# Weight pieces of the next head group tied one product earlier, and cached-key steps taken out of the changeover, in a gated-parallel decoder step on one core

## The chip, the cores and the metric

The kernel runs on one core of a Trainium2 chip. The metric is the device time of one launch in microseconds (us); the time before is the median of three timed runs, and the profile is one further execution.

## The reference

One decoder layer is applied to 1024 prompt tokens and to 64 sample tokens (8 sequences of 8 tokens, each behind a cache), all in float32:

```
u = rmsnorm(x);  [a | q | k | v | g_a | g_b] = u @ w_in
A = (multi-scale causal pooling of a, one linear map per group, scale) @ w_pa
B = (attention, 3 head groups of 4 heads, head width 64, (window, dilation) = (128,1), (512,4), (2048,16);
     q and k normed per head; the groups' outputs weighted by their softmax denominators) @ w_pb
h = x + (sigmoid(g_a) * A + sigmoid(g_b) * B) @ w_o
y = h + relu(rmsnorm(h) @ w_up)^2 @ w_down
```

The sample tokens read cached keys and values of each head group; for the group with window 2048 every sample row has 64 cached keys of its own per head. The updated caches are outputs too.

## The kernel before

All large products are made from float32 weights that are split into two parts: `panel` loads 256 columns of a weight matrix in four pieces of 256 KB into a ring of three `raw` buffers (line 119, a DMA issued by SP), and `split` writes the high part on ACT (line 108) and the remainder on DVE (line 109) into one of three `places`. A product is then three passes, 24 matmuls for a block of 128 tokens and 256 columns (`gemm`, line 147).

The attention stage runs over the head groups in the order 2, 1, 0 (line 921). Each group needs three panels, `load(0)` for q, `load(1)` for k, `load(2)` for v, and uses them for nine token blocks: block 8 holds the 64 sample rows (24 matmuls of lines 527 and 530), blocks 0 to 7 the prompt. The three places hold exactly one group's q, k and v, so the next group's q panel overwrites the q weights now in use, and so on. Products are written as (group, block, j) with j = 0, 1, 2 for q, k, v. In groups 2 and 1 the last two blocks go together, in the order (6,0), (7,0), (6,1), (7,1), (6,2), (7,2); the next group begins with blocks 8 and 0: (8,0), (0,0), (8,1), (0,1), (8,2), (0,2).

`load(j, after)` ties the split of each of the four pieces behind a named product of TensorE (`behind_pe`). A raw buffer comes free when its piece is split, and the SP queue issues its DMAs in the order in which they stand, so a DMA whose buffer isn't free holds those behind it. The order of PE is written out by hand; that of the other engines and of SP is made by a scheduler from the program.

Beside the products runs the work on the cached keys and values of group 2's sample rows: `sample_own_keys` is a generator, and each call of `own_step` (line 969) takes it one step on. A step issues the two DMAs of a piece of 256 KB (`pck` for keys, `pcv` for values, a ring of two buffers, line 719), four multiplications on POOL (line 733 or 757) and sums on DVE (lines 735, 760, 761). It needs 35 calls; groups 1 and 0 offer 19 each, one behind each product or pair of products of a prompt block. After the attention come the gate products (`pga`, `pgb`), whose panels `ga`, `gb` use the same ring and places, then output projection and feed-forward (`ph`, `pz`, `py`), which run from about 400 us of the span to its end.

Other names: `nat` are token blocks copied into order for group 0; `qs`, `wq`, `wrow` are small operands loaded at the start of group 1; `ms` and `mr` are the head norms (sum on DVE line 549, power on POOL line 550), with which ACT scales q and k (line 555) before PE transposes them (`tqg`, line 570); `sg` are scores, `smg` the exponentials (ACT line 596), `tpg` their transposes, `pog` the products with v, `ocg` their copies (line 620).

```
            load(0, (h, 6, 1), (h, 7, 1), (h, 6, 2), (h, 6, 2))
            load(1, (h, 6, 2), (h, 7, 2), (h, 7, 2), (h, 7, 2))
```

stand before a group's loop (h is the group before it), and `load(2, ...)` behind the products (8,0) and (0,0).

Of the kernel before, what the change touches and what calls it, by code (L numbers as in the profile page):

```python
# [32 lines left out]
def decoder_step(ctx, tc, i, o):  # L33
# [78 lines left out]
    def panel(src, name, between=None, after=None):  # L112

        n = src.shape[1]
        wt = places[:, place[0] % 3]
        place[0] += 1
        for a in range(0, n, 512):
            raw = rr(wp, [P, 512], F32, name=f"raw_{name}_{a}", tag="raw", bufs=3)
            dma(raw, src[:, a:a + 512])
            if between is not None:  # L120
                between(a // 512)
            ins = split(wt[:, 0, a:a + 512], wt[:, 1, a:a + 512], raw)
            if after is not None:
                behind_pe(ins, after[a // 512])
        throttle.append(ins)
        return wt
# [257 lines left out]
    def flush():  # L384
        while later:
            later.pop(0)()
# [36 lines left out]
    def pool_branch():  # L423
        res = []
        for g in range(4):
            yield from pooling(g, res)
            if g == 3:
                soon(lambda: (behind_pe(dma_st(o["pool_prompt"].rearrange("g p t -> p g t"), ends)),
                              behind_pe(dma_st(o["pool_sample"].rearrange("g p b t -> p g (b t)"), states))))
            start(pool_linear(g, *res[g]), ("p", g), now=True)  # L430
# [26 lines left out]
    def start(gen, tag, now=False, first=False):  # L457
        def run():
            yield from gen
            done.add(tag)  # L460
        if now:
            r = run()
            next(r)
            active.append(r)
        else:
            waiting.insert(0 if first else len(waiting), run())
# [18 lines left out]
    def qkv_tiles(name, sample):  # L485
        qk = rr(ap1, [P, 512], F32, name=f"qk{name}", tag="qk", bufs=2)
        if sample:
            return qk, ap1.tile([P, 256], F32, name=f"v{name}", tag="vs")
        return qk, rr(ap, [P, 256], F32, name=f"v{name}", tag="v", bufs=4)
# [12 lines left out]
    def in_order(blk):  # L502

        for s, copy in ((1, s_.copy), (0, v_.tensor_copy)):
            for k in range(0, KD, 2):
                t = rr(np_, [P, 2, P], F32R, name=f"nat{blk}_{s}{k}", tag=f"nat{s}{k}", bufs=1)
                copy(t.rearrange("p k (l r) -> p k l r", r=4),
                     act_t[s].rearrange("p k (r l) -> p k l r", r=4)[:, k:k + 2, blk * 32:(blk + 1) * 32, :].bitcast(F32))
                nat[s, k], nat[s, k + 1] = t[:, 0, :], t[:, 1, :]
# [381 lines left out]
    def own_step(every):  # L891
        count[0] += 1
        if count[0] % every == 0:
            if next(own_keys, True) is not None and (2, "own") not in done:
                done.add((2, "own"))
# [25 lines left out]
    for g in (2, 1, 0):  # L921
        nq = i["qk_norm"]
        if g == 1:
            assert ("p", 3) in done
            flush()
            pa.close()
            pam.close()
            ap2 = pb2.enter_context(tc.tile_pool(name="att2", bufs=1, reuse_waits="tile"))
            sp1 = psm.enter_context(tc.tile_pool(name="smp1", bufs=1, side="right", reuse_waits="tile"))
            np_ = psm2.enter_context(tc.tile_pool(name="nat", bufs=1, side="right", reuse_waits="tile"))  # L930
            sp = psm2.enter_context(tc.tile_pool(name="smp2", bufs=1, side="right", reuse_waits="tile"))
            osm = ap2.tile([P, 3, 4, 66], F32, name="osm")

            for a in range(2):
                v_.memset(osm[64:, a], 0.0)
                v_.memset(osm[64:, a, :, 64], -NEG)
            qs = sp1.tile([P, 768], F32, name="qs")
            for hf in range(2):
                dma(qs[64 * hf:64 * hf + 64], new_d[2].rearrange("t b c -> (t b) c"))
            wq = sp1.tile([P, 2, 256], F32, name="wq", tag="ss")[:, 0]  # L940
            dma(wq, bass.AP(tensor=nq.tensor, offset=nq.offset + 2 * 512, ap=[[0, P], [1, 256]]))
            v_.scalar_tensor_tensor(qs[:, :256], wq, HD ** -0.5, qs[:, :256], op0=ALU.mult, op1=ALU.mult)
            own_keys = sample_own_keys(qs)
        wrow = ap1.tile([P, 256], F32, name=f"wrow{g}", tag="wrow")
        dma(wrow, bass.AP(tensor=nq.tensor, offset=nq.offset + g * 512 + 256, ap=[[0, P], [1, 256]]))
        wts = [(place[0] + j) % 3 for j in range(3)]

        def load(j, *after):
            panel(i["w_in"][2 + 3 * j + g], f"qkv{g}_{j}", after=[ends_of[a] for a in after] or None)


        if g == 2:
            load(0)
            load(1)
            load(2)
        else:
            h = g + 1
            load(0, (h, 6, 1), (h, 7, 1), (h, 6, 2), (h, 6, 2))
            load(1, (h, 6, 2), (h, 7, 2), (h, 7, 2), (h, 7, 2))
        for blks in ((8, 0), (1,), (2,), (3,), (4,), (5,)) + (((6, 7),) if g else ((6,), (7,))):  # L960
            if g == 1 and 6 in blks:
                in_order(0)
            tiles = {b: qkv_tiles(f"{g}_{b}", b == 8) for b in blks}

            for js in (((0, 1), (2,)) if blks[0] in (1, 2, 3, 4, 5) else ((0,), (1,), (2,))):
                for b in blks:
                    qkv_part(g, wts, b, f"{g}_{b}", tiles[b], js)
                    if g < 2 and b < 8:
                        own_step(1)
                    if 2 in js:  # L970
                        (sample_block if b == 8 else prompt_block)(g, b, *tiles[b])
                if g == 2 and 2 in js and 8 in blks:
                    start(pool_branch(), "p", now=True)
                if g < 2 and 0 in js and 8 in blks:
                    load(2, (g, 8, 0), (g, 0, 0), (g, 0, 0), (g, 0, 0))


    while (2, "own") not in done:
# [327 lines left out]
```

## Time and profile before

| what | value |
|---|---|
| time, median of 3 runs | 1546.94 us (1546.55 to 1548.58) |
| profiled execution | 1541.33 us, span 1539.6 us |
| granted TensorE clock, mean over the span | 0.996 |
| HBM read, written | 155.54 MB, 65.10 MB |
| DMA issues of qkv weight pieces | 36 of 256 KB |
| cached pieces `pck`, `pcv` | 32 issues each, 256 KB |

The profiled execution was 5.61 us shorter than the median of the timed runs. Rows of a timeline give the start and the length in us, the engine, the line and operation, the tile written and those read, and in brackets how long the engine stood idle before it and what released it. `SPq` is the issue queue of SP. PE is TensorE's matmul, PEld its weight load.

### The profile page before, as it was taken

Reading aid. Unit: us, or ns where it says so; the run is one execution under the profiler, and the core shown is the slowest. Engines: PE = TensorE matmul, PEld = TensorE weight load, DVE = VectorE, ACT = ScalarE, POOL = GpSimd, SP = SyncE. Lnnn points to the kernel's source line nnn. Section 1 sums busy time; section 2 is a strip of 40 time slices with the busy share of each in tenths; the row PEclk is TensorE's granted clock in tenths of the full one; section 3 lists DMA queues with packets and bytes.
Section 4 is the critical chain, followed back from the end, with each engine's and each line's share of the span. In section 5 each row is a group of like instructions: output and inputs, shape, how many; then the busy total and the mean of one; then the engine's idle time right before and its main releaser. Section 6 shows DMA issues by size and latency. Waiting matters only on the chain.

```text
span 1539.6 us, 25519 instructions
## 1 busy us (share of the span) xinstructions
PE 1518.6 (99%) x9785; PEld 1473.3 (96%) x9785; DVE 880.1 (57%) x1948; ACT 521.0 (34%) x1613; POOL 202.5 (13%) x245
## 2 busy tenths in 40 slices
PE   9999899899999999999999999999999999999998
PEld 8989788778999999999999999999999999999998
DVE  7655555868745434344575555555555555655556
ACT  8567655677853232222341111111111211112100
POOL 1611256555100000010010000000000000000000
PEclk9999899999999999999999999999999999999999
DMA  5312676765344453584231331312312213223002
GB/s 199 105 51 73 183 180 167 215 163 136 108 144 161 153 173 108 172 253 169 73 107 54 107 100 60 106 65 95 106 61 99 100 64 109 75 89 106 29 7 116
DMA packets 104535, 178.64 MB, mean 116 GB/s; under 512 B 16919, under 2 KB 69725, under 8 KB 103198
## 3 DMA queue, kind: packets, MB, share of 16 engines
q1 hardware_dynamic: 98302, 126.70, 26.6%
q0 software_dynamic: 6112, 50.33, 9.7%
q8 instruction: 76, 1.25, 0.3%
q14 instruction: 45, 0.37, 0.1%
HBM read 155.54 MB, written 65.10 MB: 143 GB/s over the span
## 4 chain that ended last, share of the span: by engine, by line
PE 92%; DMA 3%; DVE 2%; ACT 1%; SPq 1%; issue 1%; POOL 0%; DVEq 0%; POOLq 0%; ACTq 0%
PE py L147 25%; PE pz L147 24%; PE pgb L147 6%; PE ph L147 6%; PE pqk L147 6%; PE pga L147 5%; PE pv L147 4%; PE pa L147 3%; PE a L261 3%; PE pb L147 2%; DMA raw_qkv<-in_w_in_dram 1%; PE pq L147 1%; PE pk L147 1%; PE pog0b L617 1%; PE sg0b L586 1%
## 5 line engine op out<-in xcount | busy, mean ns | idle before, releaser
L147 PE MATMUL pz<-act,places 128*128 128x384 f32 (+1 forms) x2304 | 382.4, 326 | 0.0
L147 PE MATMUL py<-z,places 128*128 128x384 f32 (+1 forms) x2304 | 381.6, 327 | 0.0
L147 PEld LDWEIGHTS pz<-act,places 128*128 128x128 f32 x2304 | 379.5, 188 | 0.4
L147 PEld LDWEIGHTS py<-z,places 128*128 128x128 f32 x2304 | 379.7, 188 | 0.0
L1193 DVE TENSOR_TENSOR y<-y,py 128x384 f32<-128x384 f32 (+1 forms) x360 | 188.3, 531 | 112.9 <-PE py L147 112.0
L1175 ACT ACTIVATE z<-r 128x384 fp32r<-128x384 f32 (+1 forms) x96 | 48.7, 509 | 323.3 <-DVE r L1174 323.3
L1174 DVE SCALAR_TENSOR_TENSOR r<-pz,rbh 128x384 f32<-128x384 f32 (+1 forms) x96 | 51.2, 535 | 172.5 <-PE pz L147 172.5
L1204 POOL DMA_DIRECT2D out_kv_sample_dram<-in_cache_kv_dram x44 | 21.8, 496 | 933.7 <-ACT places L108 912.4
L108 ACT ACTIVATE places<-raw_u 128x512 fp32r<-128x512 f32 x64 | 38.4, 627 | 266.9 <-PE py L147 260.1
L147 PE MATMUL pga<-act,places 128*128 128x384 f32 (+1 forms) x576 | 98.0, 328 | 0.0
L147 PE MATMUL pgb<-act,places 128*128 128x384 f32 (+1 forms) x576 | 97.8, 326 | 0.0
L147 PE MATMUL ph<-act,places 128*128 128x384 f32 (+1 forms) x576 | 95.9, 327 | 0.0
L147 PEld LDWEIGHTS pgb<-act,places 128*128 128x128 f32 x576 | 95.4, 188 | 0.0
L147 PEld LDWEIGHTS ph<-act,places 128*128 128x128 f32 x576 | 94.8, 188 | 0.3
L147 PEld LDWEIGHTS pga<-act,places 128*128 128x128 f32 x576 | 94.6, 188 | 0.3
L550 POOL TENSOR_TENSOR mr<-ms,mhalf 128x4 f32<-128x4 f32 (+2 forms) x39 | 49.6, 1273 | 107.6 <-DVE ms L549 102.0
L147 PE MATMUL pqk<-places,act 128*128 128x512 f32 x240 | 60.7, 402 | 0.0
L1177 DVE TENSOR_TENSOR z<-q,z 128x384 fp32r<-128x384 f32 (+1 forms) x96 | 51.3, 535 | 8.1
L109 DVE TENSOR_TENSOR places<-raw_d,places 128x512 fp32r<-128x512 f32 x64 | 41.4, 689 | 22.7 <-ACT places L108 22.6
L147 PEld LDWEIGHTS pqk<-places,act 128*128 128x128 f32 x240 | 44.5, 191 | 9.8 <-issue 0.2
L733 POOL TENSOR_TENSOR pck<-pck,qs 128x256 f32<-128x256 f32 x64 | 47.3, 770 | 43.5 <-DMA pck<-in_cache_kv_dram 16.6
L1176 DVE TENSOR_TENSOR q<-r 128x384 f32<-128x384 f32 (+1 forms) x96 | 51.3, 535 | 2.7
(296 smaller groups left out, 2039.7 us busy)
## 6 DMA issues: line engine op xcount, KB each, us to landing
out_kv_sample_dram<-in_cache_kv_dram POOLq DMA_DIRECT2D x36, 960.0 KB, 5.8
raw_u<-in_w_up_dram SPq DMA_DIRECT2D x64, 256.0 KB
raw_d<-in_w_down_dram SPq DMA_DIRECT2D x64, 256.0 KB
raw_qkv<-in_w_in_dram SPq DMA_DIRECT2D x36, 256.0 KB
pck<-in_cache_kv_dram SPq DMA_DIRECT2D x32, 256.0 KB
pcv<-in_cache_kv_dram SPq DMA_DIRECT2D x32, 256.0 KB
out_kv_sample_dram<-in_cache_kv_dram POOLq DMA_DIRECT2D x8, 1008.0 KB, 5.4
kts<-in_kT_dram SPq DMA_DIRECT2D x20, 256.0 KB
```

Of the source, the lines that this page charges most:

```text
L108: ins = s_.activation(dst_hi, src, AF.Copy)
L109: v_.tensor_tensor(dst_lo, src, dst_hi.bitcast(F32), op=ALU.subtract)
L147: last_mm[0] = t_.matmul(out, lhs(a, k), rhs(b, k), start=(j == 0), stop=(j == len(terms) - 1))
L261: last_mm[0] = t_.matmul(pts[m][:, :n], wt[:, a, kk, m * P:(m + 1) * P], act4[b][kk][:, :, part4(c)], start=(p == 0 and kk == 0), stop=(p ...
L550: g_.tensor_tensor(r[:n, :H], ms[:n, :H], mhalf[:n, :H], op=ALU.pow)
L733: behind_pe(g_.tensor_tensor(t[:, n], t[:, n], qs[:, :256], op=ALU.mult))
L1174: v_.scalar_tensor_tensor(r[:, :n], pzs[m][:, :n], 0.0, rbh[:, c0:c0 + n], op0=ALU.max, op1=ALU.mult)
L1175: s_.activation(z[:, m, 0, :n], r[:, :n], AF.Square)
L1176: v_.tensor_tensor(q[:, :n], r[:, :n], r[:, :n], op=ALU.mult)
L1177: v_.tensor_tensor(z[:, m, 1, :n], q[:, :n], z[:, m, 0, :n].bitcast(F32), op=ALU.subtract)
L1193: v_.tensor_tensor(yc, yc, py[:, :n], op=ALU.add)
L1204: ins = g_.dma_start(d, a)
```

## The change

Three things are altered, all in the loop over the groups.

- The pieces of q and k are tied to earlier products: the first piece of q to (7,0), the product directly behind which its place comes free, and the others one place or so ahead of where they were.
- `load(2)`, the v panel, is called behind (8,0), ahead of the product (0,0), and its first two pieces are tied to the group before's last product (7,2), the others to (8,0).
- Three of the 19 calls of `own_step` in group 1 are left out, those behind (7,1), (6,2) and (7,2). The generator then needs every call that group 0 has: before, its last three came behind block 6 of group 0, now behind block 7.

```
-            load(0, (h, 6, 1), (h, 7, 1), (h, 6, 2), (h, 6, 2))
-            load(1, (h, 6, 2), (h, 7, 2), (h, 7, 2), (h, 7, 2))
+            load(0, (h, 7, 0), (h, 6, 1), (h, 6, 1), (h, 7, 1))
+            load(1, (h, 7, 1), (h, 6, 2), (h, 6, 2), (h, 7, 2))
...
-                    if g < 2 and b < 8:
+                    if g < 2 and b < 8 and (g, b, js) not in ((1, 7, (1,)), (1, 6, (2,)), (1, 7, (2,))):
                         own_step(1)
+                    if g < 2 and b == 8 and 0 in js:
+                        load(2, (h, 7, 2), (h, 7, 2), (g, 8, 0), (g, 8, 0))
...
-                if g < 2 and 0 in js and 8 in blks:
-                    load(2, (g, 8, 0), (g, 0, 0), (g, 0, 0), (g, 0, 0))
```

What this does to the queues is seen at three places. First the SP queue at the change from group 2 to group 1, behind the small loads `wq` and `wrow`; `raw_qkv_2` are the pieces of v, `raw_qkv_0` those of the group after next (rows with - stood there before, rows with + stand there now):

```order
 L941 DMA wq<-in_qk_norm_dram 128x256
 L945 DMA wrow_1957<-in_qk_norm_dram 128x256
-L719 DMA pck_2091<-in_cache_kv_dram 64x4x256 x2
-L119 DMA raw_qkv_2_0_2094<-in_w_in_dram 128x512
-L119 DMA raw_qkv_2_512_2098<-in_w_in_dram 128x512
-L119 DMA raw_qkv_2_1024_2102<-in_w_in_dram 128x512
-L719 DMA pck_2197<-in_cache_kv_dram 64x4x256
-L694 DMA o_d_84<-ocg2b_2078 128x264
-L719 DMA pck_2197<-in_cache_kv_dram 64x4x256
+L119 DMA raw_qkv_2_1024_2044<-in_w_in_dram 128x512
+L119 DMA raw_qkv_2_1536_2048<-in_w_in_dram 128x512
+L719 DMA pck_2107<-in_cache_kv_dram 64x4x256 x2
```

Before, all four pieces of v stood behind `wrow` and a piece of cached keys, and the fourth behind three further loads; now the first two stand ahead of `wq` (directly behind the last piece of k), and the other two directly behind `wrow`.

Then ACT at the change from group 1 to group 0, from the copy of the transposed exponentials `pTg1b` on. Before:

```order
L608 COPY pTg1b_1_3658<-tpg1b_1_3653 128x512
L572 ACTIVATE qkTg1b_3660<-tqg1b_3661,wqk 128x128 x2
L546 ACTIVATE qk_8_3598,ms_8_0_3621<-pq_8_3602 64x64 x4
L108 ACTIVATE places<-raw_qkv_2_0_3735 128x512
L108 ACTIVATE places<-raw_qkv_2_512_3739 128x512
L555 ACTIVATE qk_8_3598<-pq_8_3602,mr_8_0_3622 64x64 x4
L108 ACTIVATE places<-raw_qkv_2_1024_3743 128x512
L620 COPY ocg1b_3715<-pog1b_3706 128x256
```

And in the changed kernel:

```order
L608 COPY pTg1b_1_3633<-tpg1b_1_3628 128x512
L108 ACTIVATE places<-raw_qkv_2_1024_3652 128x512
L572 ACTIVATE qkTg1b_3635<-tqg1b_3636,wqk 128x128 x2
L546 ACTIVATE qk_8_3573,ms_8_0_3596<-pq_8_3577 64x64 x4
L108 ACTIVATE places<-raw_qkv_2_1536_3656 128x512
L555 ACTIVATE qk_8_3573<-pq_8_3577,mr_8_0_3597 64x64 x4
L620 COPY ocg1b_3706<-pog1b_3697 128x256
```

Three splits of v stood between the copy and `ocg1b`; now two do, and the first two pieces are split ahead of the copy.

Last POOL at the end of group 0, where `pcv` are the last pieces of cached values and `mr` the powers for the head norms of blocks 6 and 7 (0 for q, 1 for k). Before:

```order
L757 TENSOR_TENSOR pcv_4986<-pcv_4986,sc 128x256 x4
L550 TENSOR_TENSOR mr_6_0_5021<-ms_6_0_5020,mhalf 128x4
L757 TENSOR_TENSOR pcv_5071<-pcv_5071,sc 128x256 x4
L550 TENSOR_TENSOR mr_6_1_5104<-ms_6_1_5103,mhalf 128x4
L550 TENSOR_TENSOR mr_7_0_5266<-ms_7_0_5265,mhalf 128x4
L550 TENSOR_TENSOR mr_7_1_5328<-ms_7_1_5327,mhalf 128x4
```

And in the changed kernel:

```order
L550 TENSOR_TENSOR mr_6_1_5077<-ms_6_1_5076,mhalf 128x4
L757 TENSOR_TENSOR pcv_5123<-pcv_5123,sc 128x256 x4
L757 TENSOR_TENSOR pcv_5212<-pcv_5212,sc 128x256 x2
L550 TENSOR_TENSOR mr_7_0_5247<-ms_7_0_5246,mhalf 128x4
L757 TENSOR_TENSOR pcv_5212<-pcv_5212,sc 128x256 x2
L757 TENSOR_TENSOR pcv_5285<-pcv_5285,sc 128x256 x4
L550 TENSOR_TENSOR mr_7_1_5318<-ms_7_1_5317,mhalf 128x4
```

The last three pieces now stand between the norms of block 6 and block 7, and the last of all directly ahead of `mr_7_1`. On SP that last piece is issued behind `raw_ga` pieces of the gate weights, where before all cached pieces were ahead of them.

## Prediction

> **What bounds the kernel now.** I read the page first, then the waits of TensorE, then the timelines of PE, SP, ACT and DVE where those waits lie, and last short windows with the granted clock.
>
> ```profile
> span 1539.6 us, 25519 instructions
> PE 1518.6 (99%) x9785; PEld 1473.3 (96%) x9785; DVE 880.1 (57%) x1948; ACT 521.0 (34%) x1613; POOL 202.5 (13%) x245
> ```
>
> PE is busy for 99% of the span. The change alters no product, so it can win only where PE stands idle or runs slowly, 21.0 us of idle time (1539.6 - 1518.6) and whatever the clock adds. Who ends the waits of PE:
>
> ```profile
> PE pv L530 <- DVE places L109: 5.5, 4, 3.0
> PE pq L530 <- DVE places L109: 1.9, 2, 1.2
> PE tps L817 <- DVE pxs L811: 1.6, 1, 1.6
> PE sg1b L586 <- ACT ocg1b L620: 1.5, 1, 1.5
> PE pv L527 <- ACT places L108: 1.1, 1, 1.1
> ```
>
> The columns are the total in us, the number of waits and the longest. The first, second and fifth rows are waits for weights (8.5 us), all in products of block 8. Where they lie, by the timeline of PE at the change from group 2 to 1:
>
> ```profile
> 166.71 0.36 PE L527 MATMUL pk<-places,smp_t 128*128 128x256 f32 x1
> 168.76 0.71 PE L586 MATMUL sg2b<-qkTg2b 64*128 64x128 f32 x8
> 169.40 3.14 PE L147 MATMUL pk<-places,act 128*128 128x256 f32 x24
> 173.62 0.38 PE L527 MATMUL pv<-places,smp_t 128*128 128x256 f32 x1 [1.08 <-ACT places L108]
> 181.83 0.47 PE L530 MATMUL pv<-places,smp_t 128*64 128x256 f32 x1 [2.95 <-DVE places L109]
> 184.45 4.66 PE L147 MATMUL pv<-places,act 128*128 128x256 f32 x24
> 188.95 0.38 PE L605 MATMUL tpg2b<-cst,smg2b 128*128 128x128 f32 x2
> ```
>
> The sample rows' product with k takes 2.05 us (166.71 to 168.76); the one with v starts late and is drawn out. The product (0,2) behind it takes 4.66 us where (0,1) took 3.14. Short windows tell why:
>
> ```profile
> 176.00:177.00 1.00, 0.52 (x4) 0.48 (x4) 0.56 (x2) 1.00 (x5) 0.36 (x1) 1.00 1.20 219
> 178.00:179.00 1.00, 0.87 (x4) 0.58 (x3) 0.23 (x1) 0.55 (x6) 0.04 (x1) 0.50 1.17 321
> 187.00:188.00 1.00, 1.00 (x7) 1.00 (x6) 0.00 (x0) 0.00 (x0) 0.00 (x0) 0.53 0.00 0
> ```
>
> Behind the busy times of the five engines stands the granted clock: full until 177, half from 178 to almost 188. So the late v weights cost twice, by the wait and by about 10 us at half clock. From the end of (0,1) at 172.54 (169.40 + 3.14) to 188.95 pass 16.41 us. The same work at full clock is the sample product 2.05, scores 0.64 (168.76 to 169.40), a transposition 0.38 and 3.14, together 6.21. The excess is 10.2 us, 6.6 of it waiting.
>
> Why the pieces came late, on SP, ACT and DVE:
>
> ```profile
> 150.58 8.63 SPq L119 DMA_DIRECT2D raw_qkv<-in_w_in_dram  x5
> 163.17 1.67 SPq L939 DMA_DIRECT2D qs<-new_d  x2
> 164.94 0.53 SPq L941 DMA_DIRECT2D wq<-in_qk_norm_dram  x1
> 165.99 1.35 SPq L719 DMA_DIRECT2D pck<-in_cache_kv_dram  x2
> 167.44 3.11 SPq L119 DMA_DIRECT2D raw_qkv<-in_w_in_dram  x3
> 174.62 7.50 SPq L119 DMA_DIRECT2D raw_qkv<-in_w_in_dram  x4
> 172.94 0.63 ACT L108 ACTIVATE places<-raw_qkv 128x512 fp32r<-128x512 f32 x1 [3.21 <-DMA raw_qkv<-in_w_in_dram]
> 180.42 0.63 ACT L108 ACTIVATE places<-raw_qkv 128x512 fp32r<-128x512 f32 x1 [1.87 <-DMA raw_qkv<-in_w_in_dram]
> 168.60 0.43 DVE L942 SCALAR_TENSOR_TENSOR qs<-wq,qs 128x256 f32<-128x256 f32 x1 [1.41 <-DMA wq<-in_qk_norm_dram]
> ```
>
> The first piece of v is issued at 167.44, ACT has it at 172.94 (5.50 later); the fourth is issued at 174.62 and split from 180.42 (5.80 later). Nothing is computed late: the issue order is late.
>
> **The change part by part.**
>
> *v pieces, group 2 to 1.* Two pieces move ahead of `qs` and `wq`; their buffers come free with the splits of k behind (6,2), so they leave by about 159, the end of the row of five (150.58 + 8.63), and have over 12 us until 172.5. The other two take the place of the cached piece at 165.99, and the next slot. How long do they travel? `wq` took 3.66 us from issue to use (164.94 to 168.60), the v piece 5.50 with 512 KB of cached keys ahead of it, which now come behind. I take 4.4, nearer to `wq`: landed at 170.4 and 170.9, split on ACT (0.63 each, in turn) by 171.7. The remainder on DVE stands behind four score operations there and comes some 1 us after that, 172.7 or later; PE needs the third piece about halfway through its 2.05 us. I charge a wait of 0.8. At 5.5 the wait is 2 us; at 3.66 none. A wait below 1.2 us has not halved the clock at the other change (below), so the slow stretch goes: gain 10.2 - 0.8 = **9.4 us**. Lower end: 2 us waited and the 3.6 us of slow clock kept, 4.6; upper end 10.2.
>
> The cached piece is now issued behind all four pieces of v, about 1 us later; POOL multiplies it behind (0,1) in any case, from 172.5, so that costs nothing unless it lands after 173.
>
> [...] Here the half clock began between 177 and 178, before the longest wait (2.95, up to 181.83), so shorter ones in a row sufficed (6.6 - 2.95 = 3.6 together); it ended some 6 us after PE ran again. [...]
>
> *q, k and v pieces, group 1 to 0.* PE's waits there:
>
> ```profile
> 280.34 0.33 PE L530 MATMUL pq<-places,smp_t 128*64 128x256 f32 x1 [1.18 <-DVE places L109]
> 281.69 0.33 PE L530 MATMUL pq<-places,smp_t 128*64 128x256 f32 x1 [0.68 <-DVE places L109]
> 294.02 0.71 PE L586 MATMUL sg1b<-qkTg1b 64*128 64x128 f32 x6 [1.52 <-ACT ocg1b L620]
> 301.77 0.28 PE L817 MATMUL tps<-cst,pxs 128*32 128x128 f32 x1 [1.62 <-DVE pxs L811]
> 292.00:294.00 2.00, 0.50 (x6) 0.29 (x2) 2.00 (x3) 1.59 (x8) 2.00 (x3) 1.00 0.43 145
> ```
>
> The clock stays at 1.00 beside the 1.52 us wait. The two waits for q (1.86) go: the last q piece is now tied to (7,1) instead of (6,2) and is split before the v products. The wait for `ocg1b` arose because ACT, which takes its work in order, stood at splits of v; two of these are now done before, so I take 1.0 of 1.52. `pxs` was late behind DVE's splits and the sums of three own-key steps; with these gone I take 0.8 of 1.62. Together **3.7 us**. Ends: 5.0 (all four waits) and, as no row shows what the changed order of ACT and DVE makes late, -2.0, one more wait of the size of 1.5 to 1.6 and some.
>
> *Three steps of cached work moved to block 7 of group 0.* Their sums and multiplications (no more than before in number) come later, where none of the five waits of the list lies. The place to watch is POOL:
>
> ```profile
> 385.00 2.86 POOL L757 TENSOR_TENSOR pcv<-pcv,sc 128x256 f32<-128x256 f32 x4
> 400.75 1.01 POOL L550 TENSOR_TENSOR mr<-ms,mhalf 128x4 f32<-128x4 f32 x1 [5.62 <-DVE ms L549]
> 393.71 5.00 SPq L119 DMA_DIRECT2D raw_ga<-in_w_in_dram  x4
> 402.58 0.92 ACT L555 ACTIVATE qk<-pk,mr 128x64 f32<-128x64 f32 x4
> 410.33 0.61 PE L570 MATMUL tqg0b<-cst,qk 128*128 128x128 f32 x4
> POOL pcv L757 <- DMA pcv<-in_cache_kv_dram: 13.4, 6, 3.8
> ```
>
> The power `mr_7_1` ran at 400.75; now the last piece's four multiplications (2.86) stand ahead of it. That piece leaves behind three of the four `raw_ga`, by about 396, and POOL's waits for such pieces reach 3.8, so it is multiplied from 400 to 403 or 404 and the power ends at 405; ACT scales block 7's keys by 406, and PE transposes them at 410.33. 4 us of cover remain. But ACT holds its exponentials' copies behind that scaling: I charge **-0.7**. Ends: 0 and -4 (cover used up and a wait of that size).
>
> *Sum*, against the profiled 1541.33 us (span 1539.6, 1.7 around it): 9.4 + 3.7 - 0.7 = 12.4, so 1528.9. The median was 5.61 us above that execution: 1546.94 - 12.4 = **1534.5**. Behind the attention stage PE runs almost without waits to the end, so what is won there stays won.
>
> **The rivals.**
>
> *The v weights still come late.* For it: the third and fourth pieces stay behind `qs`, `wq` and `wrow` on SP, which nothing has moved. [...] First term 4.6, second 1.9 (q alone), third -0.7: 5.8 won, **1541.1**. Against it: the fourth piece leaves 8 us earlier than at 174.62.
>
> *The change does nothing measurable.* The splits are tied earlier but the ring of three raw buffers, unchanged, lets pieces in at the old pace, and PE's wait moves from v to k. For it: the row of five took 8.63 us where an issue like that of `wq` takes 0.53. Against it: those five waited for splits that are now earlier. Within 3 us of before, **1545.5**.
>
> *Slower: the end of group 0.* The last six steps come one per product there. A step is a transfer up to 3.8 us, 2.86 on POOL and sums on DVE, 8 us in all with two buffers, so 4 per step against 4 to 5 us between products: the pace just holds. If each falls back by L (the issue stuck behind `raw_ga`), POOL's powers for blocks 6 and 7 fall back by 6 L, and PE waits for them after some 7 us of cover (401.76 + 0.92 to 410.33). The change is slower by over 0.2% from 6 L - 7 > 12.4 + 3.1, L over 3.8; at L = 5 PE waits 23, **1557.5**. Against it: before, POOL kept the pace through block 6.
>
> **How the numbers follow.** The forecast has a chance of 0.64, with its own range 1531.7 to 1538.5: 10.2 + 5.0 - 0 = 15.2 won at its best, 9.4 - 0.3 - 0.7 = 8.4 where new waits at the second change eat what it wins. Late v weights 0.18, nothing measurable 0.10, slower 0.08. The range that holds 8 in 10 goes over the first two cases, from 1531 (the best end less the 0.4 that the fastest run shown lies below the median) to 1542. 0.2%, or 3.1 us, is about what a measurement can tell here. Faster by more: 0.64 + 0.18 = 0.82; same 0.10; slower 0.08.
>
> **What would show it.** Right: no wait of `pv` for places over 1.5 us near 172, a granted clock of 1.00 in every window from 170 to 190, no wait of `pq` near 278, and `tqg0b` of block 7 without idle time before it. Wrong: a half clock again behind 177; PE idle at `tqg0b` or at transposes near 400 with POOL as the releaser; ACT idle for DMA at a v split while exponentials stand behind it.

## The result, and the profile after

The changed kernel takes 1531.81 us (median of four executions, 1531.40 to 1536.69) against 1546.74 us (four, 1546.08 to 1548.58): ratio 0.9919, 95% interval 0.9905 to 0.9933. Six further executions in a later comparison gave 1531.62 us, ratio 0.9923 (0.9908 to 0.9938). The forecast was 1534.5 with a range of 1531 to 1542.

The first profiled execution of the changed kernel is its longest of those four (1536.69 us). Its page, span and the line of busy times:

```profile
span 1534.8 us, 25518 instructions
PE 1519.1 (99%) x9785; PEld 1474.7 (96%) x9785; DVE 880.0 (57%) x1948; ACT 519.1 (34%) x1613; POOL 204.3 (13%) x245
```

PE stands idle for 15.7 us of the span, where it was 21.0. The waits of PE in the same execution (total in us, number, longest):

```profile
PE tcg0b L709 <- DVE ocg0b L643: 3.0, 2, 2.5
PE sg1b L586 <- ACT ocg1b L620: 1.4, 1, 1.4
PE tpg0b L605 <- ACT ocg0b L620: 1.3, 1, 1.3
...
PE pv L530 <- DVE places L109: 0.8, 1, 0.8
...
PE tpg2b L605 <- ACT smg2b L596: 0.6, 1, 0.6
```

Of the 8.5 us of waits for weights 0.8 is left. First and third stand two waits at the end of group 0, `tcg0b` (0.4 us in the kernel before) and `tpg0b` (not in its list). The timeline of PE at the change from group 2 to 1, and one row of ACT:

```profile
174.59 0.33 PE L530 MATMUL pv<-places,smp_t 128*64 128x256 f32 x1 [0.83 <-DVE places L109]
175.85 0.71 PE L605 MATMUL tpg2b<-cst,smg2b 128*128 128x128 f32 x2 [0.57 <-ACT smg2b L596]
177.44 4.34 PE L147 MATMUL pv<-places,act 128*128 128x256 f32 x24
181.75 3.02 PE L147 MATMUL pqk<-places,act 128*128 128x512 f32 x12
171.66 0.63 ACT L108 ACTIVATE places<-raw_qkv 128x512 fp32r<-128x512 f32 x1 [2.64 <-DMA raw_qkv<-in_w_in_dram]
```

The last row is ACT's: it still stood 2.64 us for the third piece of v, and the exponentials `smg2b`, for which PE waits 0.57 us, stand behind that split.

Short windows there (the number behind the five busy times is the granted clock):

```profile
176.00:177.00 1.00, 0.94 (x8) 0.65 (x9) 0.02 (x1) 1.00 (x8) 1.00 (x2) 0.88 1.16 323
177.00:178.00 1.00, 1.00 (x8) 0.78 (x6) 1.00 (x1) 1.00 (x10) 1.00 (x2) 0.50 1.19 313
178.00:179.00 1.00, 1.00 (x7) 1.00 (x6) 0.97 (x2) 0.80 (x4) 1.00 (x3) 0.50 1.09 336
179.00:180.00 1.00, 1.00 (x7) 1.00 (x7) 0.97 (x4) 0.00 (x0) 0.89 (x2) 0.50 0.96 346
180.00:181.00 1.00, 1.00 (x9) 1.00 (x9) 1.00 (x9) 0.91 (x4) 0.68 (x1) 0.91 0.39 148
```

A half clock remains: 0.12 + 3 x 0.50 + 0.09 is 1.71 us of clock missing, so 3.4 us at half instead of some 10, behind two waits of 0.83 and 0.57. The second profile of the same program (1529.25 us) has the 0.58 of `tpg2b` alone, and no slow clock there (its timeline, then a window):

```profile
174.87 0.71 PE L605 MATMUL tpg2b<-cst,smg2b 128*128 128x128 f32 x2 [0.58 <-ACT smg2b L596]
176.16 3.14 PE L147 MATMUL pv<-places,act 128*128 128x256 f32 x24
```

```profile
178.00:179.00 1.00, 1.00 (x10) 1.00 (x10) 0.96 (x3) 0.00 (x0) 0.89 (x2) 1.00 1.08 354
```

To see where time goes in kernels whose products stand in somewhat different order, I cut each span at five starts that all of them have in the timeline of PE: the first `pq` of block 8 in group 1, the first `pqk` behind block 8, the first `pq` of block 8 in group 0, the first `tqg0b`, and the first gate product `pgb`. In us:

| kernel | ahead | change 2 to 1 | rest of group 1 | change 1 to 0 | group 0 and `pga` | rest | profiled execution |
|---|---|---|---|---|---|---|---|
| before | 160.03 | 29.06 | 88.90 | 40.34 | 144.83 | 1076.44 | 1541.33 |
| changed, first profile | 159.79 | 21.96 | 89.37 | 37.70 | 150.77 | 1075.21 | 1536.69 |
| changed, second profile | 159.72 | 19.55 | 88.81 | 34.98 | 149.03 | 1075.41 | 1529.25 |

Before to second profile: 9.5 won at the first change, 5.4 at the second, 4.2 lost in group 0, 1.4 won ahead, between and behind (0.31 + 0.09 + 1.03): 12.1 in all. Between the two profiles of one program lie 7.4 us: 2.4, 2.7 and 1.7 of them in the three stretches with waits.

The loss in group 0 has its place at block 7. POOL, ACT, DVE and PE there, timelines of the first profile of the changed kernel, and then windows:

```profile
394.12 3.08 POOL L757 TENSOR_TENSOR pcv<-pcv,sc 128x256 f32<-128x256 f32 x4 [2.14 <-DVE ms L549]
397.17 1.00 POOL L550 TENSOR_TENSOR mr<-ms,mhalf 128x4 f32<-128x4 f32 x1
398.20 0.93 ACT L555 ACTIVATE qk<-pk,mr 128x64 f32<-128x64 f32 x4 [3.97 <-POOL mr L550]
392.94 0.67 DVE L760 TENSOR_TENSOR pcv<-pcv 128x512 f32<-128x512 f32 x1
394.01 0.68 DVE L761 TENSOR_TENSOR ss<-ss,pcv 128x512 f32<-128x512 f32 x1
394.61 0.41 DVE L643 TENSOR_TENSOR ocg0b<-ocg0b,olg0b 128x256 f32<-128x256 f32 x1
395.17 0.63 PE L709 MATMUL tcg0b<-cst,ocg0b 128*128 128x128 f32 x2 [2.52 <-DVE ocg0b L643]
409.76 0.66 PE L605 MATMUL tpg0b<-cst,smg0b 128*128 128x128 f32 x4 [1.32 <-ACT ocg0b L620]
```

```profile
395.00:396.00 1.00, 0.83 (x4) 0.86 (x5) 0.52 (x3) 0.00 (x0) 1.00 (x2) 0.61 0.00 1
396.00:397.00 1.00, 1.00 (x6) 1.00 (x5) 0.00 (x0) 0.00 (x0) 1.00 (x3) 0.50 0.88 231
397.00:398.00 1.00, 1.00 (x4) 1.00 (x4) 0.76 (x2) 0.00 (x0) 1.00 (x2) 0.50 0.15 46
398.00:399.00 1.00, 1.00 (x5) 1.00 (x5) 0.01 (x1) 0.80 (x4) 0.17 (x1) 0.69 0.06 8
```

The multiplications of the last cached piece (3.08) stand ahead of the power `mr_7_1`, and ACT stands 3.97 us for that power, with the copies and exponentials behind it. On DVE the sums of the moved steps (lines 760 and 761; two more ran from 386.46 and 388.26, 2.7 us in all) stand ahead of the sum `ocg0b` for which PE waits 2.52, and the clock halves behind that, for 3.4 us again (0.39 + 0.50 + 0.50 + 0.31 is 1.70 us of clock missing).

### The profile page after: what moved, and what is told of

The parts are those of the page before. It is cut to its first block, busy times and chain, and to the rows that moved or that the text cites. A ratio compares the mean times of both kernels' runs of the same rounds, so it can differ in the third digit from the quotient of the medians.

```text
span 1534.8 us, 25518 instructions
## 1 busy us (share of the span) xinstructions
PE 1519.1 (99%) x9785; PEld 1474.7 (96%) x9785; DVE 880.0 (57%) x1948; ACT 519.1 (34%) x1613; POOL 204.3 (13%) x245
## 4 chain that ended last, share of the span: by engine, by line
PE 89%; DMA 3%; DVE 3%; ACT 2%; POOL 1%; issue 1%; SPq 0%; DVEq 0%; ACTq 0%; POOLq 0%
PE py L147 25%; PE pz L147 24%; PE pgb L147 6%; PE ph L147 6%; PE pqk L147 5%; PE pga L147 5%; PE pv L147 3%; PE pa L147 3%; PE a L261 3%; PE pb L147 2%; DMA raw_qkv<-in_w_in_dram 1%; PE pq L147 1%; PE pk L147 1%; PE pog1b L617 1%; DMA olg0b<-o_d 1%
## 5 line engine op out<-in xcount | busy, mean ns | idle before, releaser
L757 POOL TENSOR_TENSOR pcv<-pcv,sc 128x256 f32<-128x256 f32 x64 | 47.6, 772 | 42.6 <-DMA pcv<-in_cache_kv_dram 16.0
```

What stands on the lines that cost most here:

```text
L757: behind_pe(g_.tensor_tensor(tv, tv, sc[:, j + n, :].unsqueeze(2).to_broadcast([P, 4, HD]), op=ALU.mult))
```

## The experiments

All are compared with the kernel before on the same chip, whose medians in the four comparisons were 1545.08, 1544.54, 1545.28 and 1545.04 us. The stretches of their profiles are in the table behind the last experiment.

**The v call alone.** Ties of q and k as before, all cached steps kept:

```
-                if g < 2 and 0 in js and 8 in blks:
-                    load(2, (g, 8, 0), (g, 0, 0), (g, 0, 0), (g, 0, 0))
+                    if g < 2 and b == 8 and 0 in js:
+                        load(2, (h, 7, 2), (h, 7, 2), (g, 8, 0), (g, 8, 0))
```

> Only the v pieces' call moves (behind product (8,0), new ties); q and k keep their old ties, all cached steps stay. Theory A: the late call of the v pieces is what the change between groups 2 and 1 lost, so this alone wins 7 to 10 us (1537 to 1540), pv waits under 1.5 us near 172. Theory B: the v pieces use the buffers that k's splits free, so without the earlier ties of k they come little earlier: 2 to 5 us won (1542 to 1545), and pv still waits about 2 us in one piece. The end of group 0 (no wait at tcg0b of 2 us) is as before by both.

Measured 1546.07 us, ratio 1.0009 (1.0000 to 1.0018): nothing won, not even the 2 us of theory B. SP's queue and the places where ACT and PE stood, with this kernel:

```profile
151.17 8.63 SPq L119 DMA_DIRECT2D raw_qkv<-in_w_in_dram  x5
166.66 1.47 SPq L119 DMA_DIRECT2D raw_qkv<-in_w_in_dram  x3
168.19 2.05 SPq L719 DMA_DIRECT2D pck<-in_cache_kv_dram  x3
170.93 1.51 SPq L719 DMA_DIRECT2D pck<-in_cache_kv_dram  x1
175.06 9.01 SPq L119 DMA_DIRECT2D raw_qkv<-in_w_in_dram  x4
182.36 0.63 ACT L108 ACTIVATE places<-raw_qkv 128x512 fp32r<-128x512 f32 x1 [3.93 <-DMA raw_qkv<-in_w_in_dram]
183.77 0.47 PE L530 MATMUL pv<-places,smp_t 128*64 128x256 f32 x1 [7.82 <-DVE places L109]
```

Three pieces of v leave together from 166.66, where it was 167.44, and the fourth at 175.06, behind the cached pieces. The waits of `pv` for weights are 8.6 us instead of 6.6, most of them one of 7.82. A call that stands earlier in the program does not put a piece earlier into a queue whose buffers are still held: ACT splits the last two pieces of k from 164.71, no earlier than before (163.65), and the fourth piece of v needs the buffer of the first, which is split at 171.02.

**The ties of q and k alone.** v and cached steps as before:

```
-            load(0, (h, 6, 1), (h, 7, 1), (h, 6, 2), (h, 6, 2))
+            load(0, (h, 7, 0), (h, 6, 1), (h, 6, 1), (h, 7, 1))
-            load(1, (h, 6, 2), (h, 7, 2), (h, 7, 2), (h, 7, 2))
+            load(1, (h, 7, 1), (h, 6, 2), (h, 6, 2), (h, 7, 2))
```

> Only the ties of the q and k pieces are one place earlier; v pieces and cached steps as before. Theory A: the two waits of pq near 280 go (1.9 us) and the pv waits near 174 to 182 stay: 1.5 to 4 us won, 1543 to 1545.5. Theory B: earlier k splits free the buffers for v as well, and the pv waits shrink too: 5 to 8 us won, 1539 to 1542.

Measured 1531.59 us, ratio 0.9919 (0.9905 to 0.9932): as much as the whole change. Theory B has the mechanism, with twice its size. SP's queue here, and what is left of the waits of `pv`:

```profile
149.93 8.62 SPq L119 DMA_DIRECT2D raw_qkv<-in_w_in_dram  x6
162.26 1.68 SPq L939 DMA_DIRECT2D qs<-new_d  x2
165.09 1.34 SPq L719 DMA_DIRECT2D pck<-in_cache_kv_dram  x2
166.52 1.02 SPq L119 DMA_DIRECT2D raw_qkv<-in_w_in_dram  x2
175.21 0.33 PE L530 MATMUL pv<-places,smp_t 128*64 128x256 f32 x1 [2.38 <-DVE places L109]
176.73 0.33 PE L530 MATMUL pv<-places,smp_t 128*64 128x256 f32 x1 [0.84 <-DVE places L109]
```

The row ahead of `qs` has six pieces instead of five, and only two are left behind `qs` instead of four, so of the twelve one more had left ahead of that row (in the first profile of the changed kernel one leaves alone at 145.10): the ring moved on by itself, with the call of v where it was.

**The steps alone.** Only the three calls of `own_step` left out:

```
-                    if g < 2 and b < 8:
+                    if g < 2 and b < 8 and (g, b, js) not in ((1, 7, (1,)), (1, 6, (2,)), (1, 7, (2,))):
```

> Only the three steps on cached keys are skipped (made up behind the last product of group 0); all pieces as before. Theory A: sums of moved steps stand among DVE's work in block 7 of group 0, so PE waits at tcg0b for ocg0b (about 2.5 us) and again at tpg0b (1.3), with a stretch at half clock: 4 to 6 us lost there, 0 to 2 won at the change 1 to 0 (the wait of tps for pxs): 2 to 6 us slower than before, 1549 to 1553. Theory B: the waits at block 7 of group 0 come from something else (the shifted splits of the gate panel); then no more than 1 us is lost, and up to 2 won: 1545 to 1548.

Measured 1542.41 us, ratio 0.9991 (0.9981 to 1.0001): unclear, and neither theory's time. Both halves of theory A's mechanism are in the profile: group 0 loses 5.2 us (150.01 against 144.83), and the change 1 to 0 wins 4.2 (36.16 against 40.34), twice what I allowed. Its waits at the end of group 0:

```profile
PE tcg0b L709 <- DVE ocg0b L643: 2.2, 2, 1.7
PE tpg0b L605 <- ACT ocg0b L620: 1.9, 1, 1.9
```

They are those of the changed kernel, though the ties of all weight pieces are as before. So the steps make them, and not the moved splits. At the change 1 to 0 the waits of `pq` for weights (1.9 us before) and of `tps` for `pxs` (1.6) are gone, with the ties of q where they were.

**All but the steps.** The changed kernel with every step kept; against it:

```
-                    if g < 2 and b < 8 and (g, b, js) not in ((1, 7, (1,)), (1, 6, (2,)), (1, 7, (2,))):
+                    if g < 2 and b < 8:
```

> The whole change of the ties and of the v call, but no step on cached keys skipped. Theory A: the loss in block 7 of group 0 (5.8 us in the profiled execution of the changed kernel) goes and nothing else is lost: 1526 to 1529, no wait of tcg0b for ocg0b over 1 us. Theory B: the skipped steps were needed at the change 1 to 0: their sums stand on DVE ahead of splits there, pv or pk waits come back, 2 to 5 us: 1529 to 1535.

Measured 1531.67 us, ratio 0.9919 (0.9907 to 0.9932). Group 0 is back at 144.93, but the change 1 to 0 takes 39.55, so theory B's time came out, though not its mechanism: the waits there are for `pTg1b` (1.70) and at the scores `pss` of the sample rows (0.84 and 0.46), not for weights. Leaving the steps out moves some us of waiting from one place to another and wins nothing.

**The changed kernel again.** No edit.

> The changed kernel once more, for a second profile of it and a closer ratio. Its first profiled execution took 1536.7 us where its other runs took 1531.4 to 1532.0. Theory A: the stretches at half clock (near 177, 286 and 396) come and go between executions; this profile, at 1531 to 1532, lacks one or more of them while the waits of tcg0b and tpg0b at the end of group 0 stay (group 0 about 149 to 150 us from the first tqg0b to the first gate product pgb, against 144.9 without skipped steps). Theory B: the waits at the end of group 0 themselves were particular to that execution, and group 0 takes 145 us here.

Measured 1531.62 us (1529.25 to 1536.82); theory A. The stretch in group 0 stays long (149.03), the clock is 1.00 throughout. Its last piece on POOL waited for its transfer, not for DVE, and the same chain followed:

```profile
387.68 2.75 POOL L757 TENSOR_TENSOR pcv<-pcv,sc 128x256 f32<-128x256 f32 x4 [2.14 <-DMA pcv<-in_cache_kv_dram]
391.43 0.93 ACT L555 ACTIVATE qk<-pk,mr 128x64 f32<-128x64 f32 x4 [3.19 <-POOL mr L550]
```

**The skipped steps made up in group 0.** The change, and:

```
+                        if (g, b, js) in ((0, 1, (2,)), (0, 2, (2,)), (0, 3, (2,))):
+                            own_step(1)
```

> The change, and the three skipped steps are made up early in group 0: a second step behind the last products of blocks 1, 2 and 3. Theory A: the end of group 0 is as with all steps kept (144.9 us from tqg0b to pgb) and the change 1 to 0 as in the changed kernel (36 to 37.7): 3 to 4 us faster than all steps kept, 1527.5 to 1529. Theory B: two steps behind one product hold up POOL's powers there (POOL waits for the piece's transfer), PE waits 1 to 3 us at each place: 1530 to 1537.

Measured 1533.47 us, ratio 0.9937 (0.9923 to 0.9951): theory B. The long waits at its end are gone, and the products of blocks 4 and 5 wait in their place, directly behind the doubled steps; group 0 takes 150.03, of which these two waits explain 2.2 us:

```profile
335.77 3.28 PE L147 MATMUL pqk<-places,nat 128*128 128x512 f32 x12 [1.55 <-ACT nat L507]
351.90 3.28 PE L147 MATMUL pqk<-places,nat 128*128 128x512 f32 x12 [0.65 <-ACT nat L507]
```

(The expectation of "made up between", below, speaks of a half clock and of blocks 2 and 3; the windows from 330 to 360 show 1.00, and the waits are in blocks 4 and 5.)

**Made up in group 1.** The change, and:

```
+                        if (g, b, js) in ((1, 1, (2,)), (1, 3, (2,)), (1, 5, (2,))):
+                            own_step(1)
```

> The same with the three steps made up in group 1, behind the last products of blocks 1, 3 and 5. Theory A: as made up in group 0, 1527.5 to 1529. Theory B: POOL and the DMA engines have less room in group 1 (share 0.7 to 0.75): waits there eat it, 1530 to 1537.

Measured 1531.74 us, ratio 0.9921 (0.9908 to 0.9934). Group 0 takes 144.73 and the change 37.07, but the rest of group 1 takes 2.2 us longer than in the kernel before (91.11 against 88.90). Theory B, near its lower end: no better than the changed kernel.

**The ties of k alone.** Against the kernel before:

```
-            load(1, (h, 6, 2), (h, 7, 2), (h, 7, 2), (h, 7, 2))
+            load(1, (h, 7, 1), (h, 6, 2), (h, 6, 2), (h, 7, 2))
```

> Of the ties only those of the k pieces are earlier; q, v and the cached steps as before. Theory A: the ring of three raw buffers is held by k's pieces, so their earlier splits let the first two v pieces out ahead of the new keys: nearly all of the gain of the q and k ties together (13.5 us), less the wait for q near 280 (1.9): 1532 to 1535. Theory B: the q pieces, split one place earlier, let k's pieces in and so are as much part of it: only half of the gain, 1537 to 1541.

Measured 1544.48 us, ratio 1.0003 (0.9994 to 1.0011): neither theory. Its one profile shows an execution of 2485.72 us at a granted clock of 0.56, whose times are not used here. In the program's order of SP the first three pieces of v stand behind `wrow` and two `pck` loads, as in the kernel before (issued there from 165.51 and 165.99, and v from 167.44). A row of the kernel before suggests why: ACT stood at the second piece of k for its transfer, so an earlier tie of that piece could not bring it forward while q's pieces, ahead of it in the ring, were tied late.

```profile
160.29 0.63 ACT L108 ACTIVATE places<-raw_qkv 128x512 fp32r<-128x512 f32 x1 [0.39 <-DMA raw_qkv<-in_w_in_dram]
```

**The ties of q alone.** Against the kernel before:

```
-            load(0, (h, 6, 1), (h, 7, 1), (h, 6, 2), (h, 6, 2))
+            load(0, (h, 7, 0), (h, 6, 1), (h, 6, 1), (h, 7, 1))
```

> Of the ties only those of the q pieces are earlier; k, v and the cached steps as before. The k pieces alone won nothing (ratio 1.0003), q and k together 13 us. Theory A: three buffers make the twelve pieces one chain; a gain needs both, since the v pieces come out when k's are split and k's when q's are: q alone wins only the waits of pq near 280, 1 to 3 us, 1541.5 to 1543.5. Theory B: q's late splits were the whole hindrance and k's follow by themselves: 1531 to 1534.

Measured 1543.05 us, ratio 0.9989 (0.9980 to 0.9998): theory A. In its profile the change 2 to 1 takes 30.36, no less than before: the last piece of q leaves earlier (four pieces leave from 149.94 where five left from 150.58, with four behind `qs` in both), but the last three of k are tied as late as before, and no piece of v leaves ahead of `qs` (three from 165.93). So q wins about 2 us, k nothing, the two together 13.5: twelve pieces pass three buffers in one order, and a later piece can't overtake an earlier one that is still tied late.

**Made up between.** The change, and the steps behind the first products of blocks 1, 3 and 5 of group 0:

```
+                        if (g, b, js) in ((0, 1, (0, 1)), (0, 3, (0, 1)), (0, 5, (0, 1))):
+                            own_step(1)
```

> The change, with the three skipped steps made up behind the first products (q and k) of blocks 1, 3 and 5 of group 0, two blocks apart, instead of behind the last products of blocks 1, 2 and 3 (1533.5, with waits for nat copies and a stretch at half clock in blocks 2 and 3). Theory A: two blocks apart POOL catches up; the waits at the end of group 0 go (144.9 us from tqg0b to pgb) and none come: 1528 to 1530. Theory B: any second step behind one product delays POOL's powers and with them the nat copies of ACT: 1531.5 to 1534.

Measured 1532.05 us, ratio 0.9916 (0.9903 to 0.9930): theory B. Group 0 takes 149.13, with waits of up to 0.7 us for `nat`.

**Further ahead.** All steps kept, and:

```
-            load(0, (h, 7, 0), (h, 6, 1), (h, 6, 1), (h, 7, 1))
-            load(1, (h, 7, 1), (h, 6, 2), (h, 6, 2), (h, 7, 2))
-                        load(2, (h, 7, 2), (h, 7, 2), (g, 8, 0), (g, 8, 0))
+            load(0, (h, 7, 0), (h, 7, 0), (h, 6, 1), (h, 6, 1))
+            load(1, (h, 7, 1), (h, 7, 1), (h, 6, 2), (h, 6, 2))
+                        load(2, (h, 7, 2), (h, 7, 2), (h, 7, 2), (g, 8, 0))
```

> All steps kept, and the ties of q, k and v still further ahead, as far as the products that free the places allow. Theory A: the pieces come in time already with the change's ties (pv waits 0.6 us in all), so little is left: 1530.5 to 1532, as all steps kept. Theory B: splits crowd on ACT and DVE ahead of the exponentials of blocks 6 and 7, and PE waits there: 1533 to 1538.

Measured 1530.25 us, ratio 0.9904 (0.9889 to 0.9919), just below theory A's range. The change 2 to 1 falls to 18.29, with no wait for weights at all. At the change 1 to 0 the waits are at the sample rows' scores and cached keys, with a half clock of 6.8 us behind them (the clock is 0.67 over 270 to 280 and 0.99 over 280 to 290, which is half from about 273.46 to 280.29); it takes 39.95:

```profile
272.20 0.44 PE L802 MATMUL pss<-kts,qSs 128*32 128x136 f32 x8 [1.83 <-issue]
274.10 0.68 PE L802 MATMUL pss<-kts,qSs 128*32 128x136 f32 x8 [1.46 <-DMA kts<-in_kT_dram]
```

**Both best parts.** The ties of "further ahead" at the change 2 to 1, those of the change at 1 to 0, steps made up with the two lines of "made up in group 1":

```
+            load(0, (h, 7, 0), *(((h, 7, 0), (h, 6, 1), (h, 6, 1)) if g else ((h, 6, 1), (h, 6, 1), (h, 7, 1))))
+            load(1, (h, 7, 1), *(((h, 7, 1), (h, 6, 2), (h, 6, 2)) if g else ((h, 6, 2), (h, 6, 2), (h, 7, 2))))
+                        load(2, (h, 7, 2), (h, 7, 2), (h, 7, 2) if g else (g, 8, 0), (g, 8, 0))
```

> Both best parts: at the change from group 2 to 1 the ties of the kernel that goes further ahead (there the stretch from the first pv of block 8 to the first pqk took 5.9 us against 8.0), at the change from 1 to 0 the ties of the change, the three skipped steps made up behind the last products of blocks 1, 3 and 5 of group 1. Theory A: the stretches add up: about 2 us less than made up in group 1 with the change's ties (1531.7), 1529 to 1530.5. Theory B: time won at one place is given back at the next wait, as steps skipped and made up were: 1531 to 1532.5, no measurable difference.

Measured 1529.41 us (1527.27 to 1529.86), ratio 0.9896 (0.9879 to 0.9912): theory A, 2.3 us below the kernel made up in group 1. Its median is the lowest of all, though its interval overlaps those of "further ahead" and of the changed kernel (0.9908 to 0.9938), and these ran in other comparisons. Its longest wait is the one for `ocg1b`, with a half clock behind it (timeline, then a window):

```profile
283.87 1.19 PE L586 MATMUL sg1b<-qkTg1b 64*128 64x128 f32 x6 [1.52 <-ACT ocg1b L620]
```

```profile
285.00:286.00 1.00, 1.00 (x5) 1.00 (x5) 0.97 (x3) 0.13 (x1) 0.83 (x2) 0.50 0.80 153
```

The stretches of the profiles, in us, as in the table above:

| kernel | ahead | 2 to 1 | rest of group 1 | 1 to 0 | group 0 | rest | profiled | median |
|---|---|---|---|---|---|---|---|---|
| v call alone | 160.62 | 29.84 | 88.55 | 45.66 | 144.86 | 1075.67 | 1547.12 | 1546.07 |
| q and k ties alone | 159.39 | 23.50 | 88.76 | 38.33 | 145.04 | 1075.58 | 1532.52 | 1531.59 |
| q ties alone | 159.40 | 30.36 | 88.52 | 41.57 | 144.68 | 1075.57 | 1541.90 | 1543.05 |
| steps alone | 159.87 | 29.94 | 88.67 | 36.16 | 150.01 | 1075.75 | 1542.41 | 1542.41 |
| all but the steps | 160.13 | 20.37 | 89.64 | 39.55 | 144.93 | 1075.28 | 1531.67 | 1531.67 |
| made up in group 0 | 160.43 | 19.69 | 88.80 | 36.78 | 150.03 | 1075.27 | 1532.76 | 1533.47 |
| made up between | 159.90 | 20.62 | 89.43 | 35.22 | 149.13 | 1075.30 | 1531.76 | 1532.05 |
| made up in group 1 | 160.19 | 20.38 | 91.11 | 37.07 | 144.73 | 1075.42 | 1530.87 | 1531.74 |
| further ahead | 160.10 | 18.29 | 89.86 | 39.95 | 144.51 | 1075.39 | 1530.08 | 1530.25 |
| both best parts | 160.13 | 18.31 | 91.59 | 37.48 | 145.10 | 1075.39 | 1529.86 | 1529.41 |

The steps show the same trade each time: left out, they win 4.2 us (steps alone) or 4.6 (second profile of the changed kernel against all but the steps) at the change 1 to 0; at the end of group 0 or in its blocks they cost 4 to 6, in group 1 about 2.

## Why the prediction was right, and where not

*The sum.* 12.4 us were forecast against the profiled execution; the second profile of the changed kernel is 12.1 below it, the first 4.6, the medians 14.9. The median came out 2.7 below the forecast, at the lower end of the likeliest case's own range (1531.7 to 1538.5); the second comparison gave 1531.62. The sum owes its good fit partly to luck. Against the second profile the first term is right, the second 1.7 too small, and 1.4 came from stretches that the sum left out; together these make up most of the 3.5 by which the third was too small a cost. And I carried over the 5.61 us between before's profile and its median, where the changed kernel's second profile lies 2.4 below its median.

*v pieces, group 2 to 1* (forecast 9.4). Measured 9.5 at full clock, 7.1 in the first profile, where 0.83 us was waited as forecast (0.8) and a half clock cost most of the rest. The last two pieces travelled longer than the 4.4 us that I took: issued from 165.55, ACT split them at 171.66 and 173.18. The size was right, and two pieces of v did leave ahead of `qs`; what moves them was put in the wrong place. I took k's earlier splits only as what frees their buffers. The v call alone wins nothing, and the ties of q and k alone bring 5.6 of the 8.7 us that all weight moves together bring at this place (29.06, 23.50, 20.37). In the medians they bring all of it: 1531.59 with the v call where it was, 1531.67 with it moved. What the call adds at this place in the profiles (3.1) is lost again ahead of it, in the rest of group 1 and at the second change (0.7, 0.9 and 1.2). Had I followed the ring back piece by piece, the twelve issues and the buffer each waits for, I would have seen that the ties of q start the chain.

*The half clock would go.* That step failed. I took from one row that waits below 1.2 us leave the clock full. In the first profile a half clock followed 0.83 and 0.57 within two us, and another, near 286, followed 1.45 us at `sg1b`; the kernel before took 1.52 us at the same place at full clock. Three such stretches, 1.7 us lost in each, are the greater part of the 7.4 us between two executions of one program. Two of the forecast's signs of being wrong so came in the first profile: the half clock behind 177, and ACT idle for a v split with exponentials behind it. A third came in part: PE idle at transposes near 400, released by DVE and ACT, with POOL's power one step behind ACT. The other signs were those of being right: no wait of `pv` over 1.5 us, none of `pq`, none at `tqg0b` of block 7.

*q, k and v pieces, group 1 to 0* (3.7). Measured 2.6 in the first profile and 5.4 in the second. The waits for q and for `pxs` went. Either part of the change removes both: they are missing in "q and k ties alone" and in "steps alone" alike, so they can't be shared out between the parts as I did. The wait for `ocg1b`, of which I took 1.0 us as won, stayed at 1.45 in the first profile and was 0.6 in the second. Without the steps left out the stretch gains only 0.8 (40.34 to 39.55), since other waits stand in it (`pTg1b`, `pss`) and 1.7 us of clock is missing; the steps alone bring 4.2, 3.5 of them by these two waits. I had given the steps a share in the 0.8 of `pxs` and no more.

*The three steps* (-0.7). The term that was mis-sized most: -4.2 and -5.9 measured, at and beyond the lower end of -4. The chain was the one named (the last piece's multiplications ahead of `mr_7_1`, ACT behind it, exponentials behind ACT). What I took for 4 us of cover, up to the transposition of block 7's keys, covered that transposition alone; the copies and exponentials behind the scaling had none. The sums on DVE, which I put where "none of the five waits of the list lies", made a wait of their own at `tcg0b`.

*The rivals.* The case without any effect did not come, and of the late v weights came only a trace: the 0.83 us of `pv` and the 0.57 us for `smg2b` in the first profile. The slower case's mechanism came at the size of 4 to 6 us instead of the 23 of its example, and the gain of the same steps at the change 1 to 0 paid for it.

*Left open.* The medians lie 14.9 apart, the profiles 4.6 and 12.1. The profiled execution of before was 3 to 6 us below its medians. The kernel with the v call alone shows half clocks near 300 that before's profile lacks:

```profile
290.00:300.00 10.00, 9.02 (x74) 8.36 (x74) 7.07 (x19) 6.99 (x34) 6.34 (x6) 0.83 0.83 238
300.00:310.00 10.00, 7.54 (x50) 6.59 (x50) 8.11 (x32) 7.17 (x40) 4.83 (x6) 0.73 0.44 129
```

No second profile of before was taken, but the granted clock of its timed executions is on record: 0.992 to 0.996 in the four comparisons, with medians of 0.993 or 0.994, against 0.996 in its profile. A thousandth of the span is 1.5 us, so those medians lack some 3 to 5 us more of clock, which is about the difference. In the second comparison before has a median clock of 0.994 and the changed kernel 0.999, so by an estimate from these some 8 of the 12.9 us between them are clock and not idle time; the sum had 3.6 us of clock in it. Why the k ties alone won nothing is argued from the order of the ring and the row of the kernel before; no profile at full clock shows it. A larger ring in the kernel before, which would test it, was not tried.

## What to carry to other kernels

When pieces pass through a small ring in one fixed order, the time of the last piece can be set by a late tie of any piece ahead of it: shift the whole chain from its first member, and test parts together, since each alone may show nothing. Work that is moved out of a crowded place has to be priced where it lands with all that queues behind it on every engine, above all in front of the last block, and "left out here, made up there" should be measured as a pair. Where a half clock can follow waits of one or two us (here 0.83 and 0.57, 1.45 and 2.52), two profiles of the same program are worth more than one: here one has three such stretches and the other none.

## What the runs showed of the hardware

In these profiles a half clock followed some short waits and not others, and it lasted one length or a multiple of it. Every half clock of the first profile lasted 3.4 us and lost 1.7: behind 0.83 + 0.57 us of waiting near 175, behind 1.45 us near 284, behind 2.52 us near 393. The long one in the kernel before, 10.24 us (177.70 to 187.94), is three times 3.413. None came behind 0.58 us, nor behind 1.71 us at `tpg0b` in the second profile, nor behind 1.52 us in the kernel before. Of the two profiles of one program the first has three such stretches, the second none (a clock of 1.00 throughout).

In the first profile the stretches start at 176.76, 285.99 and 395.21, and 109.23 and 218.45 us are 32 and 64 times 3.413: they lie on a grid of that step. Where a wait falls on the grid may count, which two executions suggest and do not prove. In "both best parts" the 1.52 us at `sg1b` lie within one stretch of the grid counted from its half clock (280.53 to 283.94, PE busy for 3.41 - 1.52 = 1.89 us), and the next stretch is at half clock; in the kernel before a border, counted on from 177.70, cuts the wait of the same length (290.34 to 293.75, PE busy for 2.16), and the clock stays full. How much idle time is enough stays open: a stretch of the grid with 3.41 - 1.04 = 2.37 us busy was followed by a half clock (the v call alone, 287.54 to 290.95), one with 3.41 - 1.14 - 0.44 = 1.83 was not (q and k ties alone, 273.35 to 276.77, counted back from the half clock that begins near 283.6). No wait in the first profile's three places reached 2.6 us, and in the 3.41 us ahead of its half clocks PE was busy for 1.95, 1.76 and 0.89 us.
